# The low parts of the gates' weights on VectorE or on GpSimd

## The chip, the core and the metric

The kernel runs on one core of a Trainium2 chip. A core has five engines that run their own instruction streams in order, each waiting for the others through semaphores: TensorE (PE in the profile, its weight loads PEld), VectorE (DVE), ScalarE (ACT), GpSimd (POOL) and SyncE (SP, which issues DMAs here). The metric is the time of one execution on the device in microseconds (us), as the median of several runs.

## The reference

One block of a hybrid network, for one sequence of 1024 tokens and 1024 channels. Cut to what matters:

```python
h = rms_norm(x, norm_mix_g)
proj = h @ w_in                                  # 1024 x 6664
(p_s5, p_sgu, p_dn_qkv, p_dn_z, p_dn_a, p_dn_b, p_dq, p_dk, p_dv, p_gate) = split(proj)
y_s5   = s5_mixer(p_s5, ...) @ w_br_s5           # linear state space scan
y_sgu  = sgu_mixer(p_sgu, ...) @ w_br_sgu        # spatial gating unit
y_dn   = gated_deltanet(p_dn_qkv, ...) @ w_br_dn # convolutions, then chunks of a recurrence
y_diff = diff_attention(p_dq, p_dk, p_dv, ...) @ w_br_diff
gates  = sigmoid(p_gate).reshape(..., 4, 1024)   # 4096 of the columns of proj
x = x + (gates[0]*y_s5 + gates[1]*y_sgu + gates[2]*y_dn + gates[3]*y_diff) @ w_out
x = x + conv_ffn(rms_norm(x, norm_ffn_g), ...)
out = rms_norm(x, norm_final_g)
```

## The kernel before

Channels lie on the partitions, tokens along the free axis in two halves of 512. Products are made in three parts to keep fp32 accuracy: a weight block and an activation are each split into a high part (`hi`, the value rounded to fp32r) and a low part (`lo`, what is left), and a tile of PSUM sums hi·hi, lo·hi and hi·lo (`mm3_steps`, L171). A matmul of 128 by 128 weights with 512 tokens is one `L92` row of the profile.

`w_in` is cut into 52 blocks of 128 columns, each of which `load_block` (L157) brings in as two halves of 128x512: a DMA on SP into `raw` (two buffers), a cast to the high part on ScalarE (L148, `copy_to`), and the subtraction `raw - hi` for the low part (L155, `split`). Blocks 20 to 51 (from `B_GATE` on) are the gates. Their high and low parts are the tiles `ghi` and `glo`, with four buffers each; the other blocks' are `whi` and `wlo`, with three. `load_in` (L203) chooses the tag, and the engine of the subtraction: GpSimd for the gates, VectorE for the others. A block is loaded when the one ahead of it is begun (`project`, L213).

The program runs in stages. In `norm_in` (0 to 90 us) the rms norm is built, for each half of the tokens: the input's split into `hhi` and `hlo` (L296, L297), the sum of squares `ssq` (L388), summed over the partitions by PE against ones, a chain of 128x4 steps on VectorE that makes 1/sqrt by Newton steps (`rsqrt`, L227, tiles `rs0…` and `rs1…`), its spreading by PE (`ps<-consts,rs1y`), and the rescaling of the input (`x`, L411). The first two gate blocks and the first delta net block are multiplied while the norm isn't known yet, and scaled afterwards (L223); `abf` (L426) is such a scaling too, of the decay and beta products, which PE then transposes (L96). Behind it come the delta net's convolutions and solve, with the state space scan (90 to 460), the projections and the gating unit (460 to 620), the differential attention (620 to 790), the merge (790 to 930), w_out and the feed-forward part.

The gate blocks serve as filler: `weave` (L113) interleaves the steps of the chains with the matmuls of gate blocks, as long as a chain's next step isn't due by an estimate of PE's time. What stands first in each engine's own queue is decided by a scheduler, which orders the instructions of each engine by an estimate of its own, with the subtraction's engine and length among its inputs. An engine runs its queue in that order.

Of the kernel before, what the change touches and what calls it, by code (L numbers as in the profile page):

```python
# [37 lines left out]
B_S5, B_SGU, B_DN, B_Z, B_DQ, B_DK, B_DV, B_GATE = 0, 2, 6, 12, 14, 16, 18, 20  # L38
# [60 lines left out]
class Builder:  # L99
# [103 lines left out]
    def load_in(self, blk):  # L203

        if blk not in self.early:
            tag, e_lo = ("g", self.nc.gpsimd) if blk >= B_GATE else ("w", self.nc.vector)
            self.early[blk] = self.load_block(self.a["w_in"][blk], e_lo=e_lo, tag=tag)
        return self.early[blk]

    def gate_ps(self):  # L210
# [1711 lines left out]
```

## Time and profile before

| | us |
|---|---|
| median of 3 runs | 1717.28 (1715.68 to 1718.93) |
| the profiled execution | 1719.06 |
| its span | 1717.3 |
| PE busy | 1641.2 (96%), 7762 instructions |
| DVE busy | 1256.2 (73%), 2265 |
| ACT busy | 678.4 (40%), 1219 |
| POOL busy | 645.1 (38%), 571 |
| mean granted clock of PE | 0.984 |

Busy time is the time in which an engine had an instruction in work; for PE the ends are modelled. An instruction that is held up in its course counts as busy for as long as it takes. In a timeline row the bracket holds the idle time of the engine just ahead of the instruction and the instruction of another engine that ended it. The granted clock is 1.00 at 2.4 GHz and 0.50 at 1.2 GHz; between two starts of neighbouring matmuls of 512 columns lie 0.23 us at the one and 0.43 us at the other.

### The profile page before, as it was taken

The page shows a single profiled execution, that of the slowest core. Times are in us where ns is not written, and L with a number is a line of the kernel's source. Part 1 is how long each engine was busy: PE and PEld are TensorE (multiplying, and loading weights), DVE is VectorE, ACT ScalarE, POOL GpSimd, SP SyncE. Part 2 cuts the span into 40 slices and gives each one's busy share as a digit, 9 for nine tenths or more (in the row PEclk, how much of TensorE's full clock was granted, in tenths as well). Part 3 has the DMA queues.
Part 4 walks back from the last instruction along what each step waited for, and adds up shares of the span by engine and source line. Part 5 has one row for each costly group of instructions (what it writes and reads, how often), then busy time and mean ns, then how long its engine had stood idle before and what let it go on. Part 6 is the DMA issues. An engine that isn't in the chain of part 4 may idle for free.

```text
span 1717.3 us, 22540 instructions
## 1 busy us (share of the span) xinstructions
PE 1641.2 (96%) x7762; PEld 1321.3 (77%) x7762; DVE 1256.2 (73%) x2265; ACT 678.4 (40%) x1219; POOL 645.1 (38%) x571
## 2 busy tenths in 40 slices
PE   7899999989999999999999999999998989999996
PEld 5686776766787877778888787788887777778886
DVE  8895966777623749795578667888878888855785
ACT  4342332212332336564213445454443434444353
POOL 2412033344310222211001425988999898300002
PEclk9899999999999999999999999999999999999998
DMA  4113222213432673414755442433344344687763
GB/s 156 66 64 90 60 83 70 90 64 78 149 130 98 137 141 90 102 50 150 275 201 172 141 141 66 143 123 128 135 142 148 135 147 148 219 306 242 246 213 104
DMA packets 137955, 233.64 MB, mean 136 GB/s; under 512 B 42785, under 2 KB 51745, under 8 KB 137329
## 3 DMA queue, kind: packets, MB, share of 16 engines
q1 hardware_dynamic: 105072, 151.26, 28.4%
q10 hardware_dynamic: 17968, 54.37, 8.7%
q0 software_dynamic: 14800, 26.58, 6.0%
q8 instruction: 61, 1.00, 0.2%
q14 instruction: 54, 0.43, 0.1%
HBM read 164.69 MB, written 66.85 MB: 135 GB/s over the span
## 4 chain that ended last, share of the span: by engine, by line
PE 68%; DVE 10%; DMA 3%; issue 3%; POOL 2%; ACT 2%; SPq 0%; DVEq 0%; POOLq 0%; ACTq 0%
PE qb L92 16%; PE pd L92 15%; PE qa L92 14%; PE pg L92 13%; PE ps L92 6%; DVE glo L155 2%; PE ps L96 1%; PE p L92 1%; DVE cg L1628 1%; DMA fr<-sd 1%; DMA fr<-gd 1%; ACT p L1029 0%; DMA raws<-in_w_dn_dram 0%; POOL x L1772 0%; DVE wlo L155 0%
## 5 line engine op out<-in xcount | busy, mean ns | idle before, releaser
L155 POOL TENSOR_TENSOR glo<-raw,ghi 128x512 fp32r<-128x512 f32 x72 | 98.3, 1368 | 361.7 <-ACT ghi L148 348.5
L92 PE MATMUL pg<-hhi,ghi 128*128 128x512 f32 x496 | 207.2, 418 | 0.0
L92 PE MATMUL pg<-hlo,ghi 128*128 128x512 f32 x496 | 198.9, 401 | 0.0
L92 PE MATMUL pg<-hhi,glo 128*128 128x512 f32 x496 | 198.8, 401 | 0.0
L92 PE MATMUL pd<-hhi,whi 128*128 128x512 f32 x312 | 128.2, 412 | 2.0 <-ACT silt L511 1.9
L92 PE MATMUL pd<-hhi,wlo 128*128 128x512 f32 x312 | 122.4, 392 | 2.0 <-DVE wlo L155 2.0
L92 PE MATMUL pd<-hlo,whi 128*128 128x512 f32 x312 | 122.2, 392 | 0.0
L148 ACT CAST ghi<-raw 128x512 fp32r<-128x512 f32 x97 | 59.9, 618 | 152.6 <-DVE cv L1629 75.8
L92 PE MATMUL qa<-xh,ghi 128*128 128x512 f32 x264 | 105.4, 399 | 14.9 <-DVE qa L1587 14.9
L92 PEld LDWEIGHTS pg<-hhi,ghi 128*128 128x128 f32 x496 | 95.1, 192 | 23.1 <-issue 6.7
L92 PEld LDWEIGHTS pg<-hlo,ghi 128*128 128x128 f32 x496 | 95.2, 192 | 19.3
L92 PEld LDWEIGHTS pg<-hhi,glo 128*128 128x128 f32 x496 | 95.5, 192 | 15.8 <-issue 0.3
L92 PE MATMUL qa<-xh,glo 128*128 128x512 f32 x264 | 104.4, 395 | 0.0
L92 PE MATMUL qa<-xl,ghi 128*128 128x512 f32 x264 | 104.3, 395 | 0.0
L92 PE MATMUL qb<-xh,whi 128*128 128x512 f32 x264 | 103.1, 391 | 1.2 <-ACT whi L148 0.8
L92 PE MATMUL qb<-xh,wlo 128*128 128x512 f32 x264 | 102.7, 389 | 0.0
L92 PE MATMUL qb<-xl,whi 128*128 128x512 f32 x264 | 102.7, 389 | 0.0
L148 ACT CAST whi<-raw 128x512 fp32r<-128x512 f32 x90 | 55.9, 621 | 89.2 <-PE pd L92 53.4
L155 DVE TENSOR_TENSOR wlo<-raw,whi 128x512 fp32r<-128x512 f32 x61 | 46.7, 767 | 39.1 <-ACT whi L148 38.9
L92 PEld LDWEIGHTS pd<-hhi,whi 128*128 128x128 f32 x312 | 58.8, 189 | 20.0 <-ACT silt L511 3.8
L1340 ACT ACTIVATE gate<-pg 128x512 f32<-128x512 f32 x62 | 37.1, 599 | 92.5 <-PE pg L92 91.8
L92 PEld LDWEIGHTS qa<-xh,ghi 128*128 128x128 f32 x264 | 50.6, 192 | 27.9 <-DVE qa L1587 17.4
(716 smaller groups left out, 4554.7 us busy)
## 6 DMA issues: line engine op xcount, KB each, us to landing
raw<-in_w_in_dram SPq DMA_DIRECT2D x104, 256.0 KB
gates<-gate ACTq DMA_DIRECT2D x32, 512.0 KB
gld<-gates ACTq DMA_DIRECT2D x32, 512.0 KB
fr<-in_w_up_dram SPq DMA_DIRECT2D x44, 256.0 KB
raw<-in_w_up_dram SPq DMA_DIRECT2D x44, 256.0 KB
gd<-cv ACTq DMA_DIRECT2D x22, 512.0 KB
raws<-in_w_dn_dram SPq DMA_DIRECT2D x44, 256.0 KB
tu<-in_w_dn_dram SPq DMA_DIRECT2D x33, 256.0 KB
```

The lines of the kernel that those rows point to most:

```text
L92: return self.nc.tensor.matmul(out, w, x, **kw)
L96: return self.nc.tensor.transpose(out, x, ident)
L148: eng.copy(out, in_)
L155: (e_lo or self.nc.vector).tensor_tensor(lo, src, hi.bitcast(F32), op=ALU.subtract)
L1340: self.nc.scalar.activation(self.gt[i][:, s], ps, AF.Tanh, scale=0.5)
L1628: v.scalar_tensor_tensor(gate, t, 1.0, gate, op0=ALU.add, op1=ALU.mult)
```

## The change

The low parts of the 32 gate blocks, 64 subtractions of 128x512, are made by VectorE instead of GpSimd. The DMA, the cast on ScalarE and all buffers stay as they were. The same function's line numbers are one less in the changed kernel from there on.

```diff
     def load_in(self, blk):
 
         if blk not in self.early:
-            tag, e_lo = ("g", self.nc.gpsimd) if blk >= B_GATE else ("w", self.nc.vector)
-            self.early[blk] = self.load_block(self.a["w_in"][blk], e_lo=e_lo, tag=tag)
+            self.early[blk] = self.load_block(self.a["w_in"][blk], tag="g" if blk >= B_GATE else "w")
         return self.early[blk]
```

`split` then takes its default, `e_lo or nc.vector`. VectorE's queue grows by 64, GpSimd's shrinks by 64, and the scheduler puts other instructions in another order too. After the merge, from w_out on, the queues are the same. Three places show how.

**VectorE, in the norm stage, at the sum of squares of the first half of the tokens.** `glo_146` and `glo_152` are the low parts of gate block 0, `glo_300` is the first of block 1, `rs0m` begins the first 1/sqrt. Before:

```order
L388 TENSOR_TENSOR ssq_225<-ssq_225,rms_sq_233 128x512
L297 SCALAR_TENSOR_TENSOR hlo_112<-x_157,cols_65,hhi_111 128x512
L388 TENSOR_TENSOR ssq_225<-ssq_225,rms_sq_236 128x512
L296 TENSOR_SCALAR hhi_111<-x_157,cols_65 128x512
L388 TENSOR_TENSOR ssq_225<-ssq_225,rms_sq_239 128x512
L297 SCALAR_TENSOR_TENSOR hlo_112<-x_157,cols_65,hhi_111 128x512
L388 TENSOR_TENSOR ssq_225<-ssq_225,rms_sq_242 128x512
L296 TENSOR_SCALAR hhi_111<-x_157,cols_65 128x512
L388 TENSOR_TENSOR ssq_225<-ssq_225,rms_sq_245 128x512
L297 SCALAR_TENSOR_TENSOR hlo_112<-x_157,cols_65,hhi_111 128x512
L318 TENSOR_SCALAR rs0m_253<-ps_248 128x4
```

and now:

```order
L387 TENSOR_TENSOR ssq_225<-ssq_225,rms_sq_233 128x512
L155 TENSOR_TENSOR glo_146<-raw_147,ghi_145 128x512
L387 TENSOR_TENSOR ssq_225<-ssq_225,rms_sq_236 128x512
L155 TENSOR_TENSOR glo_152<-raw_153,ghi_151 128x512
L387 TENSOR_TENSOR ssq_225<-ssq_225,rms_sq_239 128x512
L296 SCALAR_TENSOR_TENSOR hlo_112<-x_157,cols_65,hhi_111 128x512
L387 TENSOR_TENSOR ssq_225<-ssq_225,rms_sq_242 128x512
L295 TENSOR_SCALAR hhi_111<-x_157,cols_65 128x512
L387 TENSOR_TENSOR ssq_225<-ssq_225,rms_sq_245 128x512
L155 TENSOR_TENSOR glo_300<-raw_301,ghi_299 128x512
L317 TENSOR_SCALAR rs0m_253<-ps_248 128x4
```

Two subtractions took the places of an `hlo` and an `hhi`, which stand further back now, and a third that of the next `hlo`.

**VectorE, in the norm stage, at the second 1/sqrt chain** (`rs1m`, `rs1a`, `rs1y`; `glo_574` and `glo_580` are the low parts of gate block 2). The chain's last part before:

```order
L223 TENSOR_TENSOR pd_183<-pd_183,rt_122 128x512
L234 TENSOR_TENSOR rs1a_441<-rs1y_440 128x4
L235 SCALAR_TENSOR_TENSOR rs1a_441<-rs1a_441,rs1m_438 128x4
L236 SCALAR_TENSOR_TENSOR rs1y_440<-rs1a_441,rs1y_440 128x4
L234 TENSOR_TENSOR rs1a_441<-rs1y_440 128x4
L235 SCALAR_TENSOR_TENSOR rs1a_441<-rs1a_441,rs1m_438 128x4
L236 SCALAR_TENSOR_TENSOR rs1y_440<-rs1a_441,rs1y_440 128x4
L234 TENSOR_TENSOR rs1a_441<-rs1y_440 128x4
L235 SCALAR_TENSOR_TENSOR rs1a_441<-rs1a_441,rs1m_438 128x4
L236 SCALAR_TENSOR_TENSOR rs1y_440<-rs1a_441,rs1y_440 128x4
L411 SCALAR_TENSOR_TENSOR x_157<-x_157,cols_65,rt_122 128x512 x3
```

and now:

```order
L155 TENSOR_TENSOR glo_574<-raw_575,ghi_573 128x512
L235 SCALAR_TENSOR_TENSOR rs1y_440<-rs1a_441,rs1y_440 128x4
L155 TENSOR_TENSOR hlo_112<-x_123,hhi_111 128x512
L233 TENSOR_TENSOR rs1a_441<-rs1y_440 128x4
L222 TENSOR_TENSOR pd_183<-pd_183,rt_122 128x512
L234 SCALAR_TENSOR_TENSOR rs1a_441<-rs1a_441,rs1m_438 128x4
L235 SCALAR_TENSOR_TENSOR rs1y_440<-rs1a_441,rs1y_440 128x4
L155 TENSOR_TENSOR glo_580<-raw_581,ghi_579 128x512
L233 TENSOR_TENSOR rs1a_441<-rs1y_440 128x4
L234 SCALAR_TENSOR_TENSOR rs1a_441<-rs1a_441,rs1m_438 128x4
L235 SCALAR_TENSOR_TENSOR rs1y_440<-rs1a_441,rs1y_440 128x4
L155 TENSOR_TENSOR wlo_611<-raw_612,whi_610 128x512
```

The two subtractions stand between steps of the chain, and `wlo_611`, which stood behind `abf` before, comes right after it.

**TensorE, around the product that spreads the second 1/sqrt** (`ps_453`; `pg_483` is the second half of gate block 0, `pg_585` the first of gate block 2, `ps_508` the second half of block 1). Before:

```order
L92 MATMUL pg_483<-hhi_111,glo_152 128x512
L92 MATMUL ps_453<-consts_60,rs1y_440 128x128 x4
L92 MATMUL pg_483<-hlo_112,ghi_151 128x512
L92 MATMUL pg_483<-hhi_111,ghi_151 128x512
L92 MATMUL pg_483<-hhi_111,glo_152 128x512
L92 MATMUL pg_483<-hlo_112,ghi_151 128x512
L92 MATMUL ps_508<-hhi_111,ghi_299 128x512
```

and now:

```order
L92 MATMUL pg_483<-hhi_111,glo_152 128x512
L92 MATMUL pg_483<-hlo_112,ghi_151 128x512
L92 MATMUL pg_585<-hhi_111,ghi_573 128x512
L92 MATMUL pg_585<-hhi_111,glo_574 128x512
L92 MATMUL pg_585<-hlo_112,ghi_573 128x512
L92 MATMUL pg_585<-hhi_111,ghi_573 128x512
L92 MATMUL pg_585<-hhi_111,glo_574 128x512
L92 MATMUL pg_585<-hlo_112,ghi_573 128x512
L92 MATMUL pg_585<-hhi_111,ghi_573 128x512
L92 MATMUL pg_585<-hhi_111,glo_574 128x512
L92 MATMUL pg_585<-hlo_112,ghi_573 128x512
L92 MATMUL ps_453<-consts_60,rs1y_440 128x128 x4
```

Four matmuls of `pg_483` and nine of `pg_585` moved ahead of `ps_453`. The transposing of `abf` stood in PE's row 198 before and stands in row 211 now.

## Rows read from the trace of the kernel before

**Rows 1.** Windows by stage: us, busy us (x instructions) of each engine, PEclk, DMA, GB/s.

```profile
0.00:90.00 90.00, 73.82 (x301) 56.64 (x302) 78.93 (x192) 37.76 (x63) 26.46 (x21) 0.91 0.32 109
90.00:460.00 370.00, 350.81 (x1680) 270.42 (x1679) 283.57 (x808) 102.86 (x204) 109.14 (x131) 0.99 0.27 78
460.00:620.00 160.00, 159.66 (x819) 128.77 (x819) 70.53 (x180) 56.03 (x109) 27.27 (x32) 1.00 0.54 127
620.00:790.00 170.00, 165.44 (x957) 130.84 (x954) 137.66 (x266) 95.23 (x228) 32.08 (x33) 1.00 0.35 94
790.00:930.00 140.00, 139.87 (x651) 115.97 (x650) 86.49 (x130) 30.48 (x46) 13.17 (x10) 1.00 0.62 217
```

**Rows 2.** Costliest groups: busy us, mean ns, idle ahead of them and its releaser.

```profile
L155 POOL TENSOR_TENSOR glo<-raw,ghi 128x512 fp32r<-128x512 f32 x72 | 98.3, 1368 | 361.7 <-ACT ghi L148 348.5
...
L155 DVE TENSOR_TENSOR wlo<-raw,whi 128x512 fp32r<-128x512 f32 x61 | 46.7, 767 | 39.1 <-ACT whi L148 38.9
```

**Rows 3.** Windows of tile `glo` on POOL: us, POOL busy, PEclk, DMA, GB/s.

```profile
0.00:90.00 90.00, 9.47 (x6) 0.91 0.32 109
90.00:460.00 370.00, 40.12 (x30) 0.99 0.27 78
...
620.00:790.00 170.00, 22.59 (x17) 1.00 0.35 94
```

**Rows 4.** Timeline of PE, 23 to 72: start, us, instruction, idle ahead and releaser.

```profile
23.74 1.05 PE L92 MATMUL ps<-ones,ssq 128*128 128x1 f32 x8 [1.77 <-DVE ssq L388]
...
50.21 0.39 PE L92 MATMUL pg<-hhi,ghi 128*128 128x512 f32 x1
50.44 0.39 PE L92 MATMUL pg<-hhi,glo 128*128 128x512 f32 x1
54.19 2.05 PE L92 MATMUL ps<-consts,rs1y 128*128 128x128 f32 x8 [3.36 <-DVE rs1y L236]
...
71.36 0.62 PE L96 MATMUL ps<-consts,abf 40*128 40x40 f32 x4 [3.24 <-DVE abf L426]
```

**Rows 5.** Timeline of DVE, 16 to 60.

```profile
16.94 1.79 DVE L297 SCALAR_TENSOR_TENSOR hlo<-x,cols,hhi 128x512 fp32r<-128x512 f32 x1
18.65 1.77 DVE L388 TENSOR_TENSOR ssq<-ssq,rms_sq 128x512 f32<-128x512 f32 x1
...
20.74 0.68 DVE L388 TENSOR_TENSOR ssq<-ssq,rms_sq 128x512 f32<-128x512 f32 x1
21.35 0.74 DVE L297 SCALAR_TENSOR_TENSOR hlo<-x,cols,hhi 128x512 fp32r<-128x512 f32 x1
...
25.69 1.25 DVE L231 TENSOR_SCALAR rs0a<-rs0m 128x4 int32<-128x4 int32 x1
...
50.63 0.82 DVE L234 TENSOR_TENSOR rs1a<-rs1y 128x4 f32<-128x4 f32 x1
51.48 1.18 DVE L235 SCALAR_TENSOR_TENSOR rs1a<-rs1a,rs1m 128x4 f32<-128x4 f32 x1
...
53.09 0.16 DVE L235 SCALAR_TENSOR_TENSOR rs1a<-rs1a,rs1m 128x4 f32<-128x4 f32 x1
...
59.48 1.18 DVE L155 TENSOR_TENSOR hlo<-x,hhi 128x512 fp32r<-128x512 f32 x1 [0.51 <-ACT hhi L148]
```

**Rows 6.** Timeline of POOL, 16 to 61.

```profile
16.03 3.85 POOL L155 TENSOR_TENSOR glo<-raw,ghi 128x512 fp32r<-128x512 f32 x2 [14.91 <-ACT ghi L148]
23.93 2.98 POOL L155 TENSOR_TENSOR glo<-raw,ghi 128x512 fp32r<-128x512 f32 x2 [4.06 <-ACT ghi L148]
...
51.39 1.25 POOL L155 TENSOR_TENSOR glo<-raw,ghi 128x512 fp32r<-128x512 f32 x1
58.72 1.40 POOL L155 TENSOR_TENSOR glo<-raw,ghi 128x512 fp32r<-128x512 f32 x1 [6.07 <-ACT ghi L148]
```

**Rows 7.** Timeline of ACT, the cast of gate block 2's second half.

```profile
58.02 0.62 ACT L148 CAST ghi<-raw 128x512 fp32r<-128x512 f32 x1 [1.17 <-PE pg L92]
```

**Rows 8.** Waits: instruction and what it waited for, us in total, times, longest.

```profile
ACT ghi L148 <- PE pg L92: 27.2, 13, 6.8
```

## The prediction

> **What bounds the kernel now.** I read the windows by stage first [rows 1]. In each row the reader should set the TensorE (PE) busy time against the length of the stretch: PE is idle for 16.2 us of the first 90, 19.2 us of the next 370, 0.3 us from 460 to 620, 4.6 us from 620 to 790 and 0.1 us from 790 to 930. So from 460 to 620 and from 790 to 930 PE is the bound, and whatever VectorE (DVE) or GpSimd (POOL) win or lose there is hidden. The norm stage (0 to 90) is different: DVE is busy 78.93 us of 90 and PE's granted clock is 0.91. The stage from 90 to 460 (convolutions, delta net, S5) and the attention stage (620 to 790) have a DVE that is busy 77% and 81% of the time, beside chains that PE waits for now and then. After 930 no gate weights are left, and the order of the instructions there is the same in both kernels; I count nothing.
>
> Next come the instructions that move. POOL's group of `glo` has 72 instructions at a mean of 1368 ns; the same subtraction on DVE, for `wlo`, has a mean of 767 ns [rows 2]. By stage POOL holds 6, 30, 3, 17 and (790 to 930) 10 of them, the last not shown [rows 3]; 64 in all move, the other two there belong to w_out.
>
> Last, PE's stalls in the norm stage: three, of 1.77, 3.36 and 3.24 us, each ended by a DVE instruction: the sum of squares, the second rsqrt chain, and `abf` [rows 4]. That is 8.4 of the 16.2 us, and it says that DVE sets the pace of the norm stage. A change of DVE's load there reaches the end of the kernel, since the third stall ends all that was lost before: what counts is when DVE is done with `abf`, just ahead of 71.36.
>
> **Part 1: what DVE gets back.** While POOL runs a `glo`, DVE's instructions take longer [rows 5, 6]. POOL's first pair runs from 16.03 to 19.88; the `hlo` at 16.94 takes 1.79 us where the next takes 0.74, and the `ssq` at 18.65 takes 1.77 where the next takes 0.68. The pair from 23.93 to 26.91 covers a 128x4 step of 1.25 us; such a step takes 0.16 at 53.09. The one from 51.39 to 52.64 covers steps of 0.82 and 1.18, and the one from 58.72 an `hlo` of 1.18 instead of 0.68. The excess: 1.05 + 1.09 + 1.09 + 0.66 + 1.02 + 0.50 = 5.41 us, all on DVE ahead of `abf`. With POOL free of these six `glo`, it is returned.
>
> The Trainium skill, page "SBUF — State Buffer", section "Who interferes with whom", says that DVE and GpSimd hold a shared port pair exclusively for a whole instruction, and that a DVE instruction with two SBUF inputs contends with a GpSimd one that reads SBUF. The trace agrees in kind for the `hlo` and `ssq`, but 5.41 us of excess stand against 9.47 us of POOL's `glo`; if each `glo` held DVE up for its full length, the sum of part 2 would be 3.66 − 9.47 = −5.8 us. The rule also speaks against the change: the moved subtraction reads two SBUF tensors, and may now be held up itself by what POOL keeps.
>
> **Part 2: what DVE gets.** Six `glo` now stand on DVE ahead of `abf`. Start to start, such an instruction costs 0.61 us (from the `ssq` at 20.74 to the next instruction at 21.35), so 6 × 0.61 = 3.66 us. A seventh added instruction, a `wlo` that now stands ahead of the last `x` updates, I cost at nothing: it falls where DVE waits for PE and ACT after the second rsqrt chain; without that cover it costs 0.61. The numbers of the `x`, `hhi`, `hlo` and `ssq` instructions ahead of `abf` are the same. So DVE reaches `abf` 5.41 − 3.66 = **1.75 us earlier**. Bounds: all six fall in DVE's idle time, −5.41; or both late ones cost what the last rival says, +2.85, and two of them run beside POOL's remaining `hlo` and are stretched by 1.1 us each like the `hlo` at 16.94, together +5. I take −1.75 since the row nearest in kind, the pair of 16.03, has both in view: 2.14 back against two times 0.61.
>
> Two of the six are placed inside the second rsqrt chain (`glo_574`, `glo_580`). The second needs `ghi_579`, which in the trace is cast only at 58.02 to 58.64, four and a half us after the chain ended [rows 7], because its buffer was still read by PE. If DVE came to it in that state it would stand still, with the chain's last three steps and the `x` updates behind it. But PE's order has moved too: all of `pg_483` and nine matmuls of `pg_585` now come ahead of the chain's result, so the buffer is free about nine matmuls (9 × 0.23 = 2.1 us) before PE wants the result. I count no wait there, and at most about half a us.
>
> **Part 3: what PE does meanwhile.** Four rows of `pg_483` that stood behind the second chain's result and nine of `pg_585` now stand before it, and up to the `abf` step PE's order holds 13 matmuls more. At 0.23 us start to start [rows 4] that is 13 × 0.23 = 3.0 us of work done inside stalls of 3.36 and 3.24 us. It is a gain only if the filler that is thus used up isn't missed later, where chains need cover; I take half, **−1.5 us**. Ends: 0 and −3.0. The half-clock stretches behind the stalls I leave as they are, as the `abf` stall stays: PE arrives there even earlier.
>
> **Part 4: the later stages.** From 90 to 460, 30 `glo` on DVE cost 30 × 0.61 = 18.3 us; by the norm stage's ratio, 5.41 of 9.47 or 0.57, 0.57 × 40.12 = 22.9 us of stretch come back: net −4.6 us on DVE. In the attention stage: 17 × 0.61 = 10.4 against 0.57 × 22.59 = 12.9, net −2.5. DVE's load is about neutral, then, and a change of it reaches the end only where PE waits: 19.2 of 370 and 4.6 of 170 us. I take 4.6 × 0.052 + 2.5 × 0.027 = **−0.3 us**; as ends −4 (half of the net load is on the chain) and +4 (the same the other way: the order around the delta net's solve is new, and DVE now waits in order). POOL's loss of 64 × 1.37 = 88 us of work gains nothing by itself: it stood idle 348.5 us ahead of such instructions, waiting for their casts [rows 2].
>
> **The sum:** −1.75 − 1.5 − 0.3 = −3.55 us. The profiled execution took 1719.06 us (1717.3 of span, 1.8 around it), 1.8 over the median of the runs, 1717.28; taken off the median it gives **1713.7 us**, 0.21% less. A measurement of this kernel can tell about 0.2%, 3.4 us, from no change, so the forecast sits on that edge.
>
> **Rivals.** (a) Nothing to be measured. PE is idle for 40 us of the 930, and the filler taken forward is missed later: part 3 is worth 0, part 2 gives −1.75, part 4 +1: 1716.5 us. For it: PE busy in four of five stages at 94% or more. Against: stalls of the norm stage end on DVE.
>
> (b) Slower: DVE waits in order. POOL could wait for `ghi` at no cost; DVE cannot, since behind its `glo` stand the steps of the delta net's solve and of the softmax. The place is the stretch 90 to 460 and the attention stage, where 47 of the 66 stand; the price is ACT's own waiting for a free buffer, 27.2 us in 13 waits, the longest 6.8 [rows 8]. It decides once more than about two of these fall ahead of a step that PE waits for: two of the longest cost 13.6, less the 3.55 gives +10, two of the mean 4.2 give +0.6. About half way, 1722 us. For it: DVE is the busiest engine but PE there. Against: PE's idle time is small, so most chains have slack.
>
> (c) A larger gain: all the 5.41 us come back (the six `glo` fall in DVE's idle time), part 3 holds whole, and part 4 gives −4: −12.4, 1705 us. By the rule of the Trainium skill's page above of whole instructions, which the excess of 5.41 under 9.47 bears out only in part, −5.8 − 1.5 − 0.3 would give 1709.7 us; I count it in here.
>
> (d) The change doesn't do what it says: DVE's stretch is POOL's `hlo` as much as its `glo`. POOL is busy 26.46 us in the norm stage, 9.47 of them with `glo`; if the `hlo` moves under the freed instructions, part 1 gives half, 2.7, against 3.66: +1 − 1.5 − 0.3, about 1716.5 us, which goes with (a).
>
> **How the numbers follow.** Forecast (−2 to −7 us) 0.42, (a) with (d) 0.26, (b) 0.22, (c) 0.10. The forecast lies across the edge: three quarters of it, with (c), count as faster, 0.42; the rest, with (a) and (d), as the same, 0.36; (b) as slower, 0.22. The range reaches down to half of (c), 1707, and up to the middle of (b), 1722.
>
> **What would show it.** Right: in the profile after, the `ssq` at about 18 us takes 0.68, the first stall (1.77) shrinks to almost nothing, the second (3.36) to under 1, `abf` ends about 1.7 us earlier, PE does 13 matmuls more before it, and DVE's busy time stays within some 5 us of what it was while POOL's falls by 88. Wrong: a DVE group `glo` whose idle time before it, ended by ACT's `ghi`, is above some 20 us, with PE stalls from 90 to 460 or 620 to 790 behind it (rival b); 128x512 instructions of DVE still at 1.8 us in the norm stage (d); or more idle PE after 90 than 24 us, with the norm stage shorter (a).

## The result and the profile after

The changed kernel takes 1695.65 us (1693.57 to 1696.46), against 1717.78 us for the kernel before: a ratio of 0.9871 (95% interval 0.9854 to 0.9888), 22 us less. Forecast were 3.6 us less, and a range that ended at 1707. The direction was right, the size was not.

Windows of stretches that hold about the same work, first of the kernel before (columns as in [rows 1]), for the norm stage, the stretch up to 460, and the attention stage:

```profile
0.00:82.00 82.00, 65.82 (x266) 50.01 (x267) 71.85 (x160) 34.09 (x58) 26.46 (x21) 0.90 0.34 114
82.00:460.00 378.00, 358.81 (x1715) 277.06 (x1714) 290.65 (x840) 106.53 (x210) 109.14 (x131) 0.99 0.26 78
...
620.00:800.00 180.00, 175.31 (x1031) 139.31 (x1029) 141.71 (x280) 98.87 (x234) 33.92 (x35) 1.00 0.34 92
```

and of the changed kernel:

```profile
0.00:76.70 76.70, 62.09 (x271) 46.57 (x272) 68.05 (x153) 32.46 (x55) 16.39 (x15) 0.98 0.37 124
76.70:443.40 366.70, 355.98 (x1720) 276.72 (x1718) 284.77 (x883) 109.15 (x214) 75.33 (x102) 0.99 0.27 80
...
602.60:777.00 174.40, 174.10 (x1031) 139.20 (x1029) 142.18 (x297) 99.49 (x234) 9.52 (x16) 1.00 0.32 90
```

The three stretches are 5.3, 11.3 and 5.6 us shorter. PE's idle time in the second falls from 19.2 to 10.7 us and in the third from 4.7 to 0.3; the rest is PE's busy time, which falls by 3.7, 2.8 and 1.2 us at about the same number of matmuls. In the norm stage these are matmuls that no longer run at half the clock behind a stall (granted clock 0.90 before, 0.98 now). In the other two the clock explains only part of it: it is 0.99 in both kernels in the second and 1.00 in the third. DVE does 43 instructions more in the second stretch and is busy 5.9 us less. Over the whole kernel DVE's busy time goes from 1256.2 to 1252.1 us and POOL's from 645.1 to 562.9.

The `glo` on DVE in the changed kernel's timeline, at the place that [rows 5] showed held up, stand between `ssq` of normal length:

```profile
17.01 0.68 DVE L155 TENSOR_TENSOR glo<-raw,ghi 128x512 fp32r<-128x512 f32 x1
17.61 0.68 DVE L387 TENSOR_TENSOR ssq<-ssq,rms_sq 128x512 f32<-128x512 f32 x1
18.22 0.68 DVE L155 TENSOR_TENSOR glo<-raw,ghi 128x512 fp32r<-128x512 f32 x1
18.82 0.68 DVE L387 TENSOR_TENSOR ssq<-ssq,rms_sq 128x512 f32<-128x512 f32 x1
...
68.12 0.67 DVE L425 TENSOR_TENSOR abf<-ps,rt 40x512 f32<-40x512 f32 x1
```

PE's stalls in the norm stage, in answer to [rows 4]. The first (1.77) is gone; these are all that is left:

```profile
49.85 0.50 PE L92 MATMUL pg<-hhi,glo 128*128 128x512 f32 x1 [1.01 <-DVE glo L155]
53.76 1.13 PE L92 MATMUL ps<-consts,rs1y 128*128 128x128 f32 x8 [1.81 <-DVE rs1y L235]
...
67.69 0.62 PE L92 MATMUL pg<-hhi,ghi 128*128 128x512 f32 x1 [3.91 <-ACT gate L1339]
```

The one at 49.85 is new: PE waits for a `glo` that DVE made in its turn. The third now ends on ACT: PE has come to the end of the free PSUM tiles of the gates, and ACT's `gate` has to read one before it is free. But `gate` itself starts right behind DVE's scaling of such a tile, so it is still DVE that PE waits for. Of DVE and of ACT:

```profile
66.32 0.69 DVE L222 TENSOR_TENSOR pg<-pg,rt 128x512 f32<-128x512 f32 x1
```

```profile
67.04 0.60 ACT L1339 ACTIVATE gate<-pg 128x512 f32<-128x512 f32 x1
```

**Where the rest came from** is best seen at one step of the attention stage of the kernel before. Timeline of POOL, of DVE and of PE there:

```profile
698.60 2.59 POOL L155 TENSOR_TENSOR glo<-raw,ghi 128x512 fp32r<-128x512 f32 x2
```

```profile
699.03 2.19 DVE L1032 TENSOR_TENSOR drl<-drl,nlam 128x1 f32<-128x1 f32 x1
701.14 0.74 DVE L1034 TENSOR_SCALAR p<-p,drl 128x1024 f32<-128x1024 f32 x1
701.92 1.28 DVE L1035 SCALAR_TENSOR_TENSOR p<-p,drl,p 128x1024 f32<-128x1024 f32 x1
...
704.38 0.16 DVE L1032 TENSOR_TENSOR drl<-drl,nlam 128x1 f32<-128x1 f32 x1
```

```profile
703.86 1.12 PE L96 MATMUL ps<-consts,p 128*128 128x128 f32 x8 [1.81 <-DVE ptl L1056]
```

A step on one element per partition takes 2.19 us instead of 0.16: it ends at 701.22, just after POOL's two `glo` at 701.19. The softmax chain behind it is late by as much, and PE stalls 1.81 us. In the changed kernel the same 32 instructions take no more than 164 ns; first before, then after (min, median and max in ns):

```profile
L1032 DVE TENSOR_TENSOR drl<-drl,nlam x32: 142/159/2190, 638.6 to 782.9; 128x1 f32<-128x1 f32 x32
```

```profile
L1031 DVE TENSOR_TENSOR drl<-drl,nlam x32: 141/153/164, 621.2 to 760.5; 128x1 f32<-128x1 f32 x32
```

I worked this out for the whole of each trace up to the merge: of every DVE instruction beside which an arithmetic POOL instruction ran, the duration less that of an undisturbed one of the same shape (the shortest fifth). This "held-up time" is 60.8 us before, of which 34.6 fall beside the gates' `glo` (5.8 in the norm stage, 18.6 to 460, 9.6 in the attention stage), and 28.4 us after, nearly all of it beside POOL's other instructions. The sums depend on which instructions are taken as undisturbed: other choices give some 60 to 72 us before and 26 to 34 after, with 33 to 41 between the kernel before and e3 below.

### The profile page after: what moved, and what is told of

It reads as the page before. It is cut to its first block, busy times and chain, and to the rows that moved or that the text cites. A ratio compares the mean times of both kernels' runs of the same rounds, so it can differ in the third digit from the quotient of the medians.

```text
span 1694.0 us, 22538 instructions
## 1 busy us (share of the span) xinstructions
PE 1631.4 (96%) x7762; PEld 1316.2 (78%) x7762; DVE 1252.1 (74%) x2329; ACT 678.8 (40%) x1219; POOL 562.9 (33%) x507
## 3 DMA queue, kind: packets, MB, share of 16 engines
q1 hardware_dynamic: 105072, 151.26, 28.5%
## 4 chain that ended last, share of the span: by engine, by line
PE 81%; DVE 10%; issue 3%; DMA 3%; POOL 2%; ACT 1%; SPq 0%; POOLq 0%; DVEq 0%; ACTq 0%
PE pd L92 21%; PE qb L92 17%; PE pg L92 16%; PE qa L92 15%; PE ps L92 8%; PE ps L96 2%; DVE glo L155 2%; PE p L92 1%; DVE cg L1627 1%; DVE x L410 1%; DMA fr<-gd 0%; POOL x L1771 0%; DVE row L676 0%; DVE osb L675 0%; DMA raw<-in_w_out_dram 0%
## 5 line engine op out<-in xcount | busy, mean ns | idle before, releaser
L92 PEld LDWEIGHTS pg<-hlo,ghi 128*128 128x128 f32 x496 | 94.1, 190 | 18.2
L155 DVE TENSOR_TENSOR glo<-raw,ghi 128x512 fp32r<-128x512 f32 x89 | 69.3, 780 | 46.1 <-ACT ghi L148 45.8
L155 POOL TENSOR_TENSOR glo<-raw,ghi 128x512 fp32r<-128x512 f32 x8 | 11.5, 1437 | 238.5 <-ACT ghi L148 238.5
```

The costliest lines, as they stand in the source:

```text
L92: return self.nc.tensor.matmul(out, w, x, **kw)
L155: (e_lo or self.nc.vector).tensor_tensor(lo, src, hi.bitcast(F32), op=ALU.subtract)
```

## The experiments

Theory A: POOL's `glo` held up DVE instructions that chains were waiting for, and the same work on DVE stands mostly where DVE would wait. Theory B: the gain is the new order, with matmuls and chain steps at better places. A third explanation was not put to a run of its own: POOL runs its queue in order too, so a `glo` also delays the steps that POOL itself makes for the chains. It is taken up behind e2. For the runs that tell them apart, the table gives the end of the same matmuls in us: the last product with `zl` (the scan's output, the end of the stretch to 460), the last `ps<-consts,rsy` (end of the attention stage), and the last of the merge.

| kernel | `zl` | `rsy` | merge |
|---|---|---|---|
| before | 462.8 | 800.3 | 942.0 |
| changed | 444.9 | 777.3 | 919.0 |
| e1: changed, POOL reads added | 458.7 | 794.5 | 936.1 |
| e2: before, POOL reads added | 475.9 | 817.6 | 959.3 |
| e3: no subtraction | 439.0 | 771.2 | 913.9 |
| e7: changed, DVE reads added | 455.9 | 798.7 | 937.6 |

**e1, the hold-ups put back without the work.** The edit of the changed kernel, in `load_block` (`gate_in` is true while a gate block is loaded, `hp` is a pool in SBUF):

```diff
             self.split(hi[:, :m, :], lo[:, :m, :], raw, e_hi, e_lo)
+            if self.gate_in:
+                for q in range(2):
+                    h2 = hi[:, 2 * q:2 * q + 2, :].bitcast(F32)
+                    self.nc.gpsimd.tensor_tensor(self.t(self.hp, [P, 2, 128], BF16, "pdup", 1), h2, h2, op=ALU.subtract)
```

> The changed kernel, with two instructions of 128x256 added on GpSimd for each half of a gate block, which read its high part twice and write to a scratch tile that nobody reads; VectorE still makes the low parts. Theory A (GpSimd's subtractions held VectorE's chain steps up, and the change took that away): the hold-ups are back, and with them most of the gain of 22 us: 1708 to 1725 us, with VectorE's busy time up by 15 us or more. Theory B (the gain is the new order: matmuls and chain steps that stand at better places): the order of TensorE is the same up to the attention stage, so 1696 us, plus or minus 4.

Measured: 1713.94 us, a ratio of 0.9976 (0.9958 to 0.9994) to the kernel before: four fifths of the gain are gone, though DVE still makes every `glo` of the gates and PE's order is that of the changed kernel up to the attention stage. By the names of the tiles the traces have DVE, ACT and POOL in the changed kernel's order too, apart from the added instructions. At `zl`, all of it under the same order of PE, 13.8 of the 17.9 us are lost again. The added instructions, min, median and max in ns:

```profile
L172 POOL TENSOR_TENSOR pdup<-ghi x128: 606/676/3832, 16.2 to 859.7; 128x256 bf16<-128x256 f32 x128
```

Held-up time is 51.8 us, 25.1 of it beside `pdup`, and DVE's busy time rises by 24.7 us to 1276.8. Theory A; theory B is out as the main cause.

**e2, a second dose on the kernel before.** The same lines in the kernel before, behind POOL's subtraction.

> The kernel before, with the same added GpSimd instructions behind GpSimd's own subtraction, so that GpSimd does the reading twice. Theory A: a second dose of hold-ups, 1728 to 1745 us. Theory B: nothing waits for GpSimd, 1718 us, plus or minus 4.

Measured: 1735.64 us, 1.0102 (1.0082 to 1.0122), 18.7 us more. Held-up time rises by 22.0 us to 82.8, so a microsecond of it costs about 0.85 us at the end (0.8 to 0.9 by the other choices). It takes no change of DVE's work or of PE's order up to the attention stage to move the time by 1%.

**POOL's own queue.** e1 and e2 lengthen it as well, so their times alone don't tell it from theory A. The kernel before has a place where it shows. Of POOL, DVE and PE:

```profile
359.71 1.28 POOL L155 TENSOR_TENSOR glo<-raw,ghi 128x512 fp32r<-128x512 f32 x1
360.95 0.74 POOL L1241 TENSOR_TENSOR sB<-sB,s5tt 128x256 f32<-128x256 f32 x1
```

```profile
361.73 1.49 DVE L1195 TENSOR_TENSOR s5tt<-s5pi,s5bc 128x256 f32<-128x256 f32 x1 [4.89 <-POOL sB L1241]
```

```profile
370.30 0.46 PE L92 MATMUL ps<-U,M 128*128 128x128 f32 x2 [3.93 <-DVE s5tt L1195]
```

The scan's `sB` stood 1.28 us behind a `glo` on POOL while DVE waited for it; DVE's next step was then held up by another `glo` (1.49 us instead of 0.41). But the waits as a whole speak against it as the main cause: up to the merge, the idle time of PE, DVE and ACT that an instruction of POOL ended is 28.8 us before, 30.4 in the changed kernel, 30.5 in e1 and 30.9 in e2, and so doesn't follow the times. That it adds a small part is not excluded.

**e3, neither engine.** `lo` is one tile of zeros for all gate blocks. Of the edit, the lines in `load_block` that do it:

```diff
-            self.split(hi[:, :m, :], lo[:, :m, :], raw, e_hi, e_lo)
+            if self.gate_in:
+                self.copy_to(self.nc.scalar, hi, raw)
+                lo = self.zero_lo.unsqueeze(1).to_broadcast([P, 4, 128])
+            else:
+                self.split(hi[:, :m, :], lo[:, :m, :], raw, e_hi, e_lo)
```

> Neither engine makes the low parts of the gates: the product with them takes a tile of zeros (that part of the gates is left out), with the same number of matmuls. Theory A: VectorE's 64 subtractions of the changed kernel lie in its gaps, so leaving them out brings little more: 1688 to 1696 us. If VectorE's load of 64 x 0.61 = 39 us counts at the end as well: 1670 to 1688 us. Theory B: the order is another one again, no number follows but that it need not be near the changed kernel's.

Measured: 1688.47 us, 0.9829 (0.9804 to 0.9855). This is what the `glo` cost in all: on POOL 28.5 us, for 37 us of held-up time (60.8 against 23.8), or 0.77 us for each (0.7 to 0.85 by the other choices); on DVE about 7 us, for 44 us of instructions, or 0.16 us for each (by the intervals of the two ratios, 7 plus or minus 5 us). The order is another again, so these are rough; still, the same 64 subtractions cost four times as much at the end where they run on the other engine. The page of e3 has DVE at 1217.1 us, 35 less than the changed kernel:

```profile
PE 1632.5 (97%) x7762; PEld 1315.3 (78%) x7762; DVE 1217.1 (72%) x2266; ACT 678.1 (40%) x1219; POOL 559.4 (33%) x507
```

**e4, e5, e6: the change by parts.** One line each in `load_in`, here e5:

```diff
-            tag, e_lo = ("g", self.nc.gpsimd) if blk >= B_GATE else ("w", self.nc.vector)
+            tag, e_lo = ("g" if blk >= B_GATE else "w"), self.nc.gpsimd if blk >= B_GATE and not B_GATE + 3 <= blk < B_GATE + 18 else self.nc.vector
```

> Of the change only the first three gate blocks (20 to 22, all in the norm stage): six subtractions on VectorE, 58 on GpSimd as before. Both theories: the gain of the norm stage in the changed kernel's trace, 5.3 us, and nothing behind it: 1712 us. If the matmuls taken forward are missed later, less: 1714 to 1717 us.

> Of the change only gate blocks 23 to 37, whose 30 subtractions stand from 90 to 460 us in the kernel before; GpSimd makes the others. Theory A: the part of the gain that the changed kernel's trace shows from there, some 11 us: 1704 to 1710 us. Theory B (what a stage gains is the work that the norm stage took forward): little without the norm stage's part, 1713 to 1718 us.

> Of the change only gate blocks 38 to 51 (from the projections on; 17 of their 28 subtractions stand in the attention stage). Theory A: the gain of the attention stage in the changed kernel's trace, 5.6 us: 1710 to 1714 us. Theory B: 1716 to 1719 us. If the three parts (first three blocks, 23 to 37, 38 to 51) are independent of each other, their gains add up to the 21 us of the whole change.

Measured: 0.9982 (0.9968 to 0.9995), 0.9940 (0.9918 to 0.9963) and 0.9972 (0.9947 to 0.9997), so gains of 3.1, 10.3 and 4.8 us, 18.2 together where the whole change has 22: within the intervals they add up. Theory B's guess for e5 (little without the norm stage's part) falls. In e4's trace the lead is 5.5 us at 85 us and 3.7, 3.4 and 3.3 us at the three steps of the table: of the 3 us of matmuls taken forward in the norm stage, some 2 were missed later.

**e7, the added reads on DVE instead.** As e1, with `nc.vector` for `nc.gpsimd`.

> The changed kernel, with the added instructions of e1 (two of 128x256 for each half of a gate block, reading the high part twice, into a scratch tile) on VectorE instead of GpSimd: 128 instructions of some 0.35 us start to start, some 45 us more work for VectorE, as much as the change itself gave it. If VectorE's load beside the chains mostly lies in its waits (what the run without subtractions says: 7 us for 64 of them): 1700 to 1706 us. If the net load counts by the idle share of TensorE, as in the prediction (about 5%): 1697 to 1699. If it counts in full where VectorE is on the chain: 1715 us and more.

Measured: 1713.91 us, 0.9973 (0.9956 to 0.999), where the changed kernel beside it had 1698.11 (0.9877): 16 us more, near the last of the three guesses and far from the one that I held likely. The added instructions hold DVE for 54.8 us:

```profile
L172 DVE TENSOR_TENSOR pdup<-ghi x128: 385/417/898, 18.1 to 861.5; 128x256 bf16<-128x256 f32 x128
```

So a second dose costs 0.3 us for each microsecond, by the medians twice the first, though at 16 plus or minus 5 us and 7 plus or minus 5 the two prices are not clearly apart. 6.3 of the 16 us are lost by the end of `abf` (75.13 against 68.79), in the norm stage, where DVE is the bound. DVE's gaps are thus no free store: they took 44 us of subtractions for 7 us, and the next 55 for 16. Not all of that is the queue: the order of PE and DVE is another one in e7, and DVE's held-up time beside POOL's other instructions is 5 to 9 us longer than in the changed kernel. That the first dose is cheap because the scheduler finds gaps for it is argued from this, not shown.

**b1 to b4: more of POOL's work on DVE.** b1 is the changed kernel with this line, b3 has the low parts of the feed-forward weights that POOL makes in `pair_weights` on DVE, b4 is both. b1:

```diff
-            self.split(self.h_hi[:, k, s], self.h_lo[:, k, s], x[:, k, :], nc.scalar, nc.vector if k % 3 == 0 else nc.gpsimd)
+            self.split(self.h_hi[:, k, s], self.h_lo[:, k, s], x[:, k, :], nc.scalar, nc.vector)
```

and b3, where `gl` is `nc.vector`:

```diff
-        add(a11, g)
+        add(a11, gl)
...
-        add(s2, g)
+        add(s2, gl)
...
-        add(s3, g)
+        add(s3, gl)
...
-        add(s4, g)
-        add(a22, g)
+        add(s4, gl)
+        add(a22, gl)
```

> The changed kernel, and the norm stage's ten low parts of the input that GpSimd still makes (hlo) also on VectorE. Theory A taken further: they hold VectorE up by 9.0 us ahead of the third stall and would cost it 10 x 0.61 = 6.1: 1692 to 1695 us. If VectorE, which is the bound there, pays their length in full and half of the hold-ups lay beside waits: 1696 to 1699 us.

> The changed kernel, and the low parts of the feed-forward weights that GpSimd makes in the first of its two products (those of the raw weights and of their sums) on VectorE. In that stage GpSimd's instructions hold VectorE up by some 89 us in the changed kernel's trace, but TensorE is idle only 36 of 787 us there, and VectorE is busy 76%. Theory A taken further: 1685 to 1695 us; if VectorE becomes the bound there: 1696 to 1710 us.

> b1 and b3 together: the norm stage's hlo and the feed-forward weights' low parts on VectorE. If both are independent, the gain of b1 (4 to 5 us over the changed kernel) on top of what b3 gives: 1681 to 1691 us where b3 gains, 1692 to 1705 us where b3 loses.

> The changed kernel again, beside the others on the same chip, as the measure for b3, b4 and e7: 1695.7 us, plus or minus 2.

Measured: b1 1690.97 us (0.9868, 0.9815 to 0.992); b3 1693.21 us (0.9860, 0.9843 to 0.9876); b4 1689.11 us (0.9831, 0.9811 to 0.985); the changed kernel beside b3 and b4 1698.11 us (0.9877, 0.9856 to 0.9898). b4 beats both kernels, with an interval that lies below that of the changed kernel. b1 and b3 by themselves are not told apart from it by their intervals; b4 against b3 is 0.29%, the 4 to 5 us expected of the norm stage's `hlo`, with intervals that overlap a little; in b4's trace `abf` ends at 65.47 us where the changed kernel has 68.79. After the merge b3 and b4 are some 6 us shorter than the changed kernel (769.1 and 769.7 us against 775.0). The pages of the changed kernel and of b4:

```profile
PE 1631.4 (96%) x7762; PEld 1316.2 (78%) x7762; DVE 1252.1 (74%) x2329; ACT 678.8 (40%) x1219; POOL 562.9 (33%) x507
```

```profile
PE 1627.3 (97%) x7762; PEld 1310.1 (78%) x7762; DVE 1297.9 (77%) x2444; ACT 672.9 (40%) x1219; POOL 397.6 (24%) x392
```

**b2: the rest beside the chains.** The changed kernel, with `ql`, `zl`, `kdec` and `RK` on DVE, by `nc.vector` for `nc.gpsimd` in five lines, of which two:

```diff
-                        self.split(hi[:, s], lo[:, s], f[:, s], nc.scalar, nc.gpsimd)
+                        self.split(hi[:, s], lo[:, s], f[:, s], nc.scalar, nc.vector)
...
-        nc.gpsimd.tensor_tensor(kdec, rk_tile[:, :, 1], sc[:, 2].unsqueeze(3).to_broadcast(S64), op=ALU.mult)
+        nc.vector.tensor_tensor(kdec, rk_tile[:, :, 1], sc[:, 2].unsqueeze(3).to_broadcast(S64), op=ALU.mult)
```

> The changed kernel, and three more of GpSimd's jobs beside the chains on VectorE: the split of the queries (ql, 8), of the scan's output (zl, 8) and the scaling of the keys (kdec, RK, 6 of 128x1024). Theory A taken further: they hold VectorE up by some 8 us from 76 to 443 us and would cost it some 20 us, more than they give, but off the chain in part: 1692 to 1700 us, better only if they fall in gaps as the gates' low parts do.

Measured: 1700.55 us, 0.9916 (0.9889 to 0.9942), by the medians of the ratios some 0.4% slower than the changed kernel (0.9871 and 0.9877), though the intervals touch. Up to `zl` it is ahead of it (442.9 against 444.9); at the end of the attention stage it is 7.3 us behind (784.6 against 777.3). Timelines of ACT, DVE and PE of b2 just before that stage:

```profile
593.82 0.62 ACT L148 CAST ghi<-raw 128x512 fp32r<-128x512 f32 x1 [10.32 <-DMA raw<-in_w_in_dram]
```

```profile
594.47 0.69 DVE L155 TENSOR_TENSOR glo<-raw,ghi 128x512 fp32r<-128x512 f32 x1 [9.56 <-ACT ghi L148]
...
598.34 0.68 DVE L155 TENSOR_TENSOR wlo<-raw,whi 128x512 fp32r<-128x512 f32 x1
```

```profile
595.53 0.50 PE L92 MATMUL pd<-hhi,whi 128*128 128x512 f32 x1 [4.27 <-ACT whi L148]
599.08 0.79 PE L92 MATMUL pd<-hhi,wlo 128*128 128x512 f32 x1 [3.05 <-DVE wlo L155]
```

ACT's cast waited 10 us for a load, DVE's `glo` waited for the cast with everything behind it, and PE stalled 7.3 us. 3.05 of these are rival (b) of the prediction as it would look; the 4.27 ahead of them end on a cast of ACT that stood behind the late one in ACT's own queue. The load itself was not slower than in the changed kernel: SP issued it at 580.28, when DVE's `wlo` had freed its buffer, and it landed 13.5 us later, among transfers that POOL had issued from 571 to 576; in the changed kernel the loads issued at 566.56 and 570.13, beside the same transfers, took 16.2 and 21.9 us, and PE did not stand still. Why the queues stand so that it did in b2 is open.

## Why the prediction was wrong

**What bounds the kernel** was read rightly: DVE in the norm stage, PE from 460 to 620 and after 790. Little moved there: the lead at `zl` is 17.9 us, at 616 us 17.4.

**Parts 1 to 3, the norm stage,** were right in mechanism and nearly in size, the size with some luck. Forecast −3.25 us; 5.3 are there at the stage's end, and e4, which has only this part, keeps 3.1 by its ratio and 3.3 to 3.7 in its trace. One of the six terms of the 5.41 was misread: the step of 0.82 at 50.63 ran beside POOL's `hlo`, not beside the `glo` that starts at 51.39, so 0.66 of the sum was not the change's to give back (in the changed kernel the step at 50.39 still takes 1.28 beside an `hlo`):

```profile
50.13 1.30 POOL L155 TENSOR_TENSOR hlo<-x,hhi 128x512 fp32r<-128x512 f32 x1 [2.07 <-ACT hhi L148]
```

`abf` ends 2.4 us earlier (68.79 against 71.21) where 1.75 was said; the `ssq` take 0.68; the first stall is gone. The second (1.81) is not under 1. The stall of 1.01 is on `glo_574`, which came late in DVE's queue, a wait of PE that the prediction had not counted; the wait of DVE for `ghi_579`, put at half a us at most, did not come, as its cast ended at 50.29 and DVE began `glo_580` at 52.46. Of the matmuls taken forward about a third held, where half was taken.

**Part 4 was the step that failed**: −0.3 us for the stages behind, where the trace has −12.6 to `zl` and −5.6 in the attention stage. The load was right: DVE's net load moved by −4.1 us over the kernel. Wrong was to net the two and to multiply by the share of time in which PE is idle, as if both were spread evenly. They have two prices. Up to the merge, time held up is paid at about 0.8 us for each (0.85 in e2, 0.77 in e3), since POOL's instruction holds what DVE has ready at that moment, and beside the chains that is often the step PE will wait for next, as the 128x1 step at 699.03. Time added as a subtraction in DVE's own queue was paid at 0.16 (e3). With these prices, 18.6 × 0.8 − 20.9 × 0.16 = 11.5 us to `zl` (20.9 us is the 30 `glo` there on DVE), and 9.6 × 0.8 − 12.3 × 0.16 = 5.7 in the attention stage, where 12.6 and 5.6 were measured. The prices stem from whole runs of the same change or its double, so this shows that the account closes, not that the prices hold elsewhere; e7 suggests that the second rises with the load.

The idle time as such misled too: 19.2 us of idle PE looked like a cap of a few us on what could be won, but 8.5 of them went, and 2.8 us of PE's busy time with them. The ends of part 4 (−4 and +4) were set from half the net load, and so the range ended 11 us too high.

**Rivals.** (a) fell: the later stages did gain. (b)'s waits came: DVE stood idle for 36 us ahead of `glo` up to the merge, in 18 waits, the longest 7.1:

```profile
DVE glo L155 <- ACT ghi L148: 36.0, 18, 7.1
```

They cost little, since e3, without any, is only 7 us faster; in b2 one of them had a part in a stall. (c) had the right side and the largest hold-up in view, but bounded part 4 by the same netted load; even it stopped at 1705. (d) fell for the `glo` (e1), though its sign is there and it names what was left: an `hlo` of DVE still takes 1.78 us at 62.25, and POOL's `hlo` held DVE up for 9 us in the norm stage, which b4 then took.

## What to carry to other kernels

Work on one engine that makes another's instructions longer is charged to whatever that other engine has ready, which beside a chain is the chain; look in the trace for small steps that take ten times their usual length, sum the excess, and where PE waits for such chains count most of it as time on the path, not its net against the moved load. That holds for the stages up to the merge: behind it, the same sum is some 90 us in the changed kernel where PE is idle for 36 us in all, so it can't all be paid at 0.8 there. Work that goes into a busy engine's own queue was cheap here while there were waits to fill (0.16) and seems to get dearer (0.3 for the second dose); an in-order wait for a late load is the risk, as in b2.

## What the runs showed of the hardware

A held-up DVE instruction does its work after the end of POOL's, however small it is itself: the 128x1 at 699.03 took 2.19 us, through the rest of one `glo` of POOL and all of the next. The Trainium skill, page "SBUF — State Buffer", section "Who interferes with whom", says that the second of two such instructions blocks until the first ends, and that a VectorE instruction with two SBUF inputs is one that contends; the trace agrees. So the whole-instruction reading that the prediction set aside holds for each instruction that is held up; that DVE would get all 9.47 us of the norm stage's `glo` back does not follow, as it held DVE up for 5.8 us.

Not every DVE instruction is held. Of those of the kernel before that began beside an arithmetic POOL instruction with enough of it left to cover their usual length (up to 800 us), 59 of the 62 of the two- or three-operand forms with all inputs in SBUF were longer than usual by more than 0.15 us, and none of the 21 with one input in PSUM. All 5 `TENSOR_SCALAR`, with their one input in SBUF, were longer too. Two with an input in PSUM, of DVE, beside a `glo` of POOL; they take 0.57 us together:

```profile
295.98 0.57 DVE L742 SCALAR_TENSOR_TENSOR state<-state,gl,ps 64x64 f32<-64x64 f32 x2
296.58 0.93 DVE L1196 TENSOR_TENSOR NB<-NB,s5tt 128x288 f32<-128x288 f32 x1
```

```profile
295.90 1.29 POOL L155 TENSOR_TENSOR glo<-raw,ghi 128x512 fp32r<-128x512 f32 x1 [2.60 <-ACT ghi L148]
```

The next one has both inputs in SBUF. It begins while POOL's `glo`, which ends at 297.19, is still running, and takes 0.93 us; the undisturbed ones of its shape take 0.45.
